# Gated-recurrence score products in blocks of 32 on quarters of TensorE's array, with the running samples' products moved behind them

## The chip, the cores and the metric

One core of a Trainium2 chip runs one program. The metric is the device time of one execution in microseconds (us); the number compared is the median of several runs. The engines are TensorE (PE, with its weight loads PEld), VectorE (DVE), ScalarE (ACT), GpSimd (POOL, all but unused here) and SyncE (SP), which issues the DMAs.

## The reference, cut to what matters

A two-layer trunk for 256 new tokens and 8 single-token running samples (264 columns in all), width 2048: layer 0 mixes with a Conformer convolution, layer 1 with an HGRN2 gated recurrence of 16 heads of 128 x 128; each layer ends in a convolutional FFN of width 5632. The change is in the recurrence:

```
G = jnp.cumsum(gc, axis=1)
decay = jnp.exp(G[:, :, None] - G[:, None, :])            # where s <= t
A = jnp.einsum('bthk,btshk,bshk->bths', qc, decay, kc)    # scores
o = jnp.einsum('bths,bshv->bthv', A, vc) + (qc * jnp.exp(G)) @ S
S_new = jnp.exp(G_last)[..., None] * S + (kc * jnp.exp(G_last - G)).T @ vc
```

For a running sample with one token it is S = f * S + k v and o = q S, followed by an RMS norm per head and a gate.

## The kernel before, in words

**Wide products.** Every weight matrix comes in tiles of 2048 x 128 (1 MB, one DMA each). ACT rounds a tile to `wh` (L137), DVE makes the rest `wl` (L149), and PE multiplies in three products per 128 rows: `wh` x high part (L179), `wh` x low part (L180), `wl` x high part (L181), each 128 x 128 by 264 columns. A call of `slot` is one such tile: 16 x 3 = 48 wide products into one PSUM bank. Four tiles (`NATIVE`) go in plain fp32 instead (L176).

**Order.** PE, ACT and DVE run exactly in the order in which the code is written. `slot` first writes its 48 products and then takes one turn of a list: functions registered with `later(n, ...)` run n turns later, first those marked `first`, then the splits of coming weights (`wh` before, `wl` after the plain functions), then those marked `last`. So what PE does in a turn stands behind that slot's wide products; what DVE and ACT do in it runs beside them.

**A head.** Heads go through three slots each: `hf` (forget gate), `hq` (query), `hi` (value); behind the heads in `GATE_AFTER` one gate slot `hg` is put in, and the seven remaining `hg` slots follow the last head. After a head's `hi` slot, `doubling` builds query/key pairs R[2], R[4], ... R[128] whose decays are taken to the middle of blocks of 2, 4, ... tokens. One turn later PE does `flip` (three transposes, L714 and L715) and `scores`: for seven levels (L750: the diagonal, then blocks of 1, 2, 4, 8, 16, 32 tokens) and four groups of 64 tokens a product of 64 keys by 64 queries, all levels side by side in `pl` (two PSUM banks); then the 128-token block (L753), two 64 x 64 products for the 64-token level (L756), and two transposes (L759), all into `pa`. A turn later `select` copies the parts of `pa` (ACT, L765 to L768), multiplies `pl` with a 0/1 mask and sums over levels (DVE, L769 and L772), and `place` copies the sums into the score matrix AT (ACT, L777). `outputs` (L800 to L804) follows a turn later.

**Samples.** `sample_state` (DVE, L792, eight instructions, interleaved with the head's norm) updates the head's states `sm` four turns behind the head's first turn, and `sample_outputs` (PE, L813, eight products of 32 columns of `alone` by 128) reads them a turn later, into one bank `pos` that all heads share. After the last head, `pos` is copied, transposed (L878), squared, summed over partitions (L886), and `sample_norm` (DVE, L891 to L894) scales it. Then `samples_gated` (L925) multiplies with the gates, and the first `ho` slot (plain fp32, L176) reads the result `o2`.

An fp32 product leaves two records in the trace, each with a weight load of its own; a transpose and a wide product leave one.

Of the kernel before, what the change touches and what calls it, by code (L numbers as in the profile page):

```python
# [8 lines left out]
F32 = mybir.dt.float32  # L9
# [3 lines left out]
ALU = mybir.AluOpType  # L13
# [4 lines left out]
P = 128  # L18
# [6 lines left out]
HEADS = 16  # L25
# [21 lines left out]
LOADS = 4  # L47
TE = 17

GATE_AFTER = (3, 4, 6, 7, 9, 10, 12, 13, 15)  # L50
# [10 lines left out]
def kernel(ctx: ExitStack, tc: tile.TileContext, a: dict):  # L61
# [6 lines left out]
    wp = ctx.enter_context(tc.tile_pool(name="wp", bufs=3))  # L68
    ps = ctx.enter_context(tc.tile_pool(name="ps", bufs=5, space=PSUM))

    def bank(name):
        return ps.tile([P, 512], F32, tag="pt", name=name)
# [86 lines left out]
    def later(slots, fn, last=False, first=False):  # L159

        todo[slots][0 if first else 2 if last else 1].append(fn)
# [452 lines left out]
    with ExitStack() as ph:  # L614
# [5 lines left out]

        mask = cst[:, P:].rearrange("p (o n) -> p o n", o=1).to_broadcast((P, 2, len(LV) * 64))
        AT = [h1.tile([P, 2, P], F32, tag=f"AT{i}", name=f"AT{i}") for i in range(2)]
        for t in AT:
            vec.memset(t[64:, :, :64], 0.0)
        gss = h1.tile([P, HEADS, NB], F32, tag="gss", name="gss")
# [115 lines left out]
        def scores(h):  # L741
            d = heads[h]
            R, qk, K = d["R"], d["qk"], d["K"]
            pl = d["pl"] = ps.tile([P, 2, 512], F32, tag="pl", name=f"pl{h}", bufs=1)
            for l, b in enumerate(LV):
                for hf in range(2):
                    for i in range(2):
                        s = (2 * hf + i) * 64
                        key, query = (qk[:, 2, :], qk[:, 0, :]) if b == 0 else (R[b][:, 1, :], R[b][:, 0, :])
                        pe.matmul(pl[i * 64 : i * 64 + 64, hf, l * 64 : (l + 1) * 64], key[:, s : s + 64], query[:, s : s + 64],  # L750
                                  start=True, stop=True)
            pa = d["pa"] = bank(f"pa{h}")
            pe.matmul(pa[:, :P], R[128][:, 1, :P], R[128][:, 0, P:SEQ], start=True, stop=True)  # L753
            for hf in range(2):
                s = hf * P
                pe.matmul(pa[:64, P + hf * 64 : P + (hf + 1) * 64], R[64][:, 1, s : s + 64], R[64][:, 0, s + 64 : s + P],  # L756
                          start=True, stop=True)
            for i, k in enumerate((K, R[128][:, 1, P:SEQ])):
                pe.transpose(pa[:, (2 + i) * P : (3 + i) * P], k, ident)  # L759

        def select(h):
            d = heads[h]
            pa, pl, W = d.pop("pa"), d.pop("pl"), AT[h % 2]
            Kt = d["Kt"] = hp.tile([P, 2, P], F32, tag="Kt", name=f"Kt{h}", bufs=1)
            act.copy(Kt, pa[:, 2 * P :].rearrange("p (i k) -> p i k", i=2))  # L765
            act.copy(W[:64, :, 64:], pa[:64, P : 2 * P].rearrange("p (o t) -> p o t", o=2))
            A1 = d["A1"] = hp.tile([P, P], F32, tag="A1", name=f"A1_{h}", bufs=1)
            act.copy(A1, pa[:, :P])  # L768
            vec.tensor_tensor(out=pl[:, :, : len(LV) * 64], in0=pl[:, :, : len(LV) * 64], in1=mask, op=ALU.mult)  # L769
            lm = pl[:, :, : len(LV) * 64].rearrange("p o (l t) -> p o t l", t=64)  # L770
            wd = heads[h]["wd"] = hp.tile([P, 2, 64], F32, tag="wd", name=f"wd{h}", bufs=1)
            vec.tensor_reduce(out=wd, in_=lm, axis=AX.X, op=ALU.add)  # L772

        def place(h):
            for i in range(2):
                r = slice(i * 64, i * 64 + 64)
                act.copy(AT[h % 2][r, :, r], heads[h]["wd"][r])  # L777

# [144 lines left out]
        def samples_gated(lo, hi):  # L923
            assert all(heads[h]["gated"] for h in range(lo, hi))
            vec.tensor_tensor(out=o2[:, lo:hi, SEQ:], in0=o2[:, lo:hi, SEQ:], in1=gss[:, lo:hi, :], op=ALU.mult)  # L925

        for name, h in HGRN:
# [9 lines left out]
            elif name == "hi":  # L937
# [10 lines left out]
                later(4, lambda h=h: sample_state_and_norm(h))  # L948
                later(5, lambda h=h: sample_outputs(h), last=True)
                later(5, lambda h=h: normed(h))  # L950
                later(6, lambda h=h: flop(h), last=True)
                later(7, lambda h=h: columns(h), first=True)
                if h == HEADS - 1:
                    later(6, sample_rows, first=True)
                    later(6, sample_columns, last=True)
                    later(7, sample_squares, first=True)
                    later(7, sample_sum, last=True)
                    later(8, sample_norm, first=True)
                    later(8, lambda: samples_gated(0, HEADS - 2), last=True)
                    later(8, lambda: samples_gated(HEADS - 2, HEADS), last=True)  # L960
# [18 lines left out]
    with ExitStack() as ph:  # L979
# [10 lines left out]

        pl = ps.tile([P, 2, 512], F32, tag="pl", name="p_y", bufs=1)
        pt = ps.tile([P, 512], F32, tag="st", name="p_ss", bufs=1)
# [9 lines left out]
        for i in range(2):  # L1002
            turn_back(i, 1, pl[:, i, :])
        steps, r = [], []
# [112 lines left out]
```

## Time and profile before

| | us |
|---|---|
| median of 3 runs | 2479.26 (2478.76 to 2480.55) |
| the profiled execution | 2478.74 |
| its span, first to last instruction | 2477.0 |
| PE busy | 2446.4 (99%) |
| DVE busy | 1759.9 (71%) |
| ACT busy | 1110.7 (45%) |
| mean granted TensorE clock | 0.996 of full |

Busy time is the union of an engine's instructions. A PE record is as long as the product's way through the array; successive products overlap, so the distance between starts, not the length, is what a product costs. The recurrence's slots run from about 1131 to 1594 us.

### The profile page before, as it was taken

Reading aid. Unit: us, or ns where it says so; the run is one execution under the profiler, and the core shown is the slowest. Engines: PE = TensorE matmul, PEld = TensorE weight load, DVE = VectorE, ACT = ScalarE, POOL = GpSimd, SP = SyncE. Lnnn points to the kernel's source line nnn. Section 1 sums busy time; section 2 is a strip of 40 time slices with the busy share of each in tenths; the row PEclk is TensorE's granted clock in tenths of the full one; section 3 lists DMA queues with packets and bytes.
Section 4 is the critical chain, followed back from the end, with each engine's and each line's share of the span. In section 5 each row is a group of like instructions: output and inputs, shape, how many; then the busy total and the mean of one; then the engine's idle time right before and its main releaser. Section 6 shows DMA issues by size and latency. Waiting matters only on the chain.

```text
span 2477.0 us, 46795 instructions
## 1 busy us (share of the span) xinstructions
PE 2446.4 (99%) x19878; PEld 2391.7 (97%) x19878; DVE 1759.9 (71%) x3087; ACT 1110.7 (45%) x1759; POOL 0.2 (0%) x4
## 2 busy tenths in 40 slices
PE   8999899999999999999999999899999999999998
PEld 7888899999999999999999999899999999999998
DVE  8999867766566567568887888657767657656655
ACT  1112645444344344345655665444444444435434
POOL 0000000000000000000000000000000000000000
PEclk9999999999999999999999999999999999999999
DMA  7444445554554554555655655455555455455453
GB/s 270 150 153 142 169 173 204 176 182 156 202 187 161 182 196 164 180 182 197 232 190 202 222 208 199 161 182 199 176 187 173 158 205 180 158 201 186 164 176 129
DMA packets 78129, 452.92 MB, mean 183 GB/s; under 512 B 8544, under 2 KB 13024, under 8 KB 39008
## 3 DMA queue, kind: packets, MB, share of 16 engines
q1 hardware_dynamic: 77920, 449.94, 51.6%
q8 instruction: 155, 2.54, 0.4%
q14 instruction: 54, 0.44, 0.0%
HBM read 436.31 MB, written 15.50 MB: 182 GB/s over the span
## 4 chain that ended last, share of the span: by engine, by line
PE 99%; DVE 1%; issue 0%; DMA 0%; ACT 0%; ACTq 0%; SPq 0%; DVEq 0%
PE p_up L181 14%; PE p_up L179 14%; PE p_up L180 14%; PE p_pw L176 10%; PE p_dn L181 7%; PE p_dn L180 7%; PE p_dn L179 7%; PE p_hi L179 1%; PE p_hg L179 1%; PE p_hf L179 1%; PE p_hq L179 1%; PE p_hf L181 1%; PE p_hg L181 1%; PE p_hq L181 1%; PE p_hi L181 1%; PE p_hi L180 1%
## 5 line engine op out<-in xcount | busy, mean ns | idle before, releaser
L179 PE MATMUL p_up<-h_ffn,wh_up 128*128 128x264 f32 x2816 | 801.1, 284 | 0.0
L181 PE MATMUL p_up<-h_ffn,wl_up 128*128 128x264 f32 x2816 | 800.7, 284 | 0.0
L180 PE MATMUL p_up<-l_ffn,wh_up 128*128 128x264 f32 x2816 | 797.5, 283 | 0.0
L149 DVE TENSOR_TENSOR wl_up<-w_up,wh_up 128x2048 fp32r<-128x2048 f32 x176 | 403.5, 2293 | 231.9 <-ACT wh_up L137 231.9
L137 ACT CAST wh_up<-w_up 128x2048 fp32r<-128x2048 f32 x176 | 335.9, 1909 | 505.9 <-PE p_up L180 446.8
L179 PEld LDWEIGHTS p_up<-h_ffn,wh_up 128*128 128x128 f32 x2816 | 530.1, 188 | 0.1
L181 PEld LDWEIGHTS p_up<-h_ffn,wl_up 128*128 128x128 f32 x2816 | 530.0, 188 | 0.0
L180 PEld LDWEIGHTS p_up<-l_ffn,wh_up 128*128 128x128 f32 x2816 | 529.6, 188 | 0.1
L181 PE MATMUL p_dn<-gh,wl_dn 128*128 128x264 f32 x1408 | 400.8, 285 | 0.0
L179 PE MATMUL p_dn<-gh,wh_dn 128*128 128x264 f32 x1408 | 400.3, 284 | 0.0
L180 PE MATMUL p_dn<-gl,wh_dn 128*128 128x264 f32 x1408 | 400.1, 284 | 0.0
L137 ACT CAST wh_dn<-w_dn 128x1408 fp32r<-128x1408 f32 x128 | 175.9, 1374 | 325.9 <-PE p_dn L180 243.8
L149 DVE TENSOR_TENSOR wl_dn<-w_dn,wh_dn 128x1408 fp32r<-128x1408 f32 x128 | 208.1, 1626 | 108.3 <-ACT wh_dn L137 108.3
L180 PEld LDWEIGHTS p_dn<-gl,wh_dn 128*128 128x128 f32 x1408 | 265.3, 188 | 0.0
L181 PEld LDWEIGHTS p_dn<-gh,wl_dn 128*128 128x128 f32 x1408 | 264.7, 188 | 0.0
L179 PEld LDWEIGHTS p_dn<-gh,wh_dn 128*128 128x128 f32 x1408 | 264.6, 188 | 0.0
L176 PE MATMUL p_pw<-xg,w_pw 128*128 128x264 f32 x960 | 213.9, 386 | 0.0
L176 PEld LDWEIGHTS p_pw<-xg,w_pw 128*128 128x128 f32 x960 | 182.4, 190 | 31.2
L567 DVE SCALAR_TENSOR_TENSOR C<-H,par,C 128x255 f32<-128x255 f32 x352 | 169.1, 480 | 6.3
L278 DVE TENSOR_TENSOR x<-x,p_dn 128x264 f32<-128x264 f32 x128 | 54.9, 429 | 111.9 <-PE p_dn L181 111.9
L561 DVE TENSOR_TENSOR H<-p_up,rstd_ffn 128x264 f32<-128x264 f32 x176 | 76.1, 432 | 78.3 <-PE p_up L181 78.3
L562 ACT ACTIVATE C<-H,par 128x264 f32<-128x264 f32 x176 | 105.5, 600 | 13.9 <-DVE H L561 13.9
(316 smaller groups left out, 4007.9 us busy)
## 6 DMA issues: line engine op xcount, KB each, us to landing
w_up<-in_up SPq DMA_DIRECT2D x176, 1024.0 KB
w_dn<-in_dn SPq DMA_DIRECT2D x128, 704.0 KB
w_pw<-in_pw SPq DMA_DIRECT2D x47, 1024.0 KB
w_hf<-in_hf SPq DMA_DIRECT2D x16, 1024.0 KB
w_hq<-in_hq SPq DMA_DIRECT2D x16, 1024.0 KB
w_hi<-in_hi SPq DMA_DIRECT2D x16, 1024.0 KB
w_hg<-in_hg SPq DMA_DIRECT2D x16, 1024.0 KB
w_ho<-in_ho SPq DMA_DIRECT2D x16, 1024.0 KB
```

The costliest lines, as they stand in the source:

```text
L137: act.copy(wh[:, :kk, :], raw[key][:, :kk, :])
L149: vec.tensor_tensor(out=wl[:, :kk, :], in0=raw.pop(key)[:, :kk, :], in1=wh.bitcast(F32)[:, :kk, :], op=ALU.subtract)
L176: pe.matmul(pt[:, :T], wh[:, k, :], full[k], start=(k == 0), stop=last)
L179: pe.matmul(pt[:, :T], wh[:, k, :], rh, start=(k == 0), stop=False)
L180: pe.matmul(pt[:, :T], wh[:, k, :], rl, start=False, stop=False)
L181: pe.matmul(pt[:, :T], wl[:, k, :], rh, start=False, stop=last)
L278: vec.tensor_tensor(out=x[n], in0=x[n], in1=pt[:, :T], op=ALU.add)
L561: vec.tensor_tensor(out=h, in0=pt[:, :T], in1=rstd, op=ALU.mult)
L562: act.activation(cc, h, AF.Identity, scale=wv[:, j, 2:3], bias=pcol("ffn_b", layer * 2 * FT + j))
L567: vec.scalar_tensor_tensor(out=cc[:, d:SEQ], in0=h[:, : SEQ - d], scalar=wv[:, j, 2 - d : 3 - d], in1=cc[:, d:SEQ], op0=ALU.mult, op1=ALU.add)
```

## The change

Scores of the diagonal and of the levels 1 to 16 are made in blocks of 32 keys by 32 queries: six levels, each eight blocks, of which four consecutive ones go to the four 32-column quarters of the array (output partitions 0, 32, 64, 96). `pl` shrinks to 384 columns in one PSUM bank, the free bank goes to the common pool (five banks to six), and mask and sum work on 384 instead of 896 columns. The 32-token level becomes four 32 x 32 products into free columns of `pa` (quarters 0 and 2), the 64-token level four products of 32 keys by 64 queries (one to a quarter). Behind them stand the samples' products of the head before (`sample_outputs(h - 1)`), then the 128-token product and the transposes. `select` and `place` have more, smaller copies. The last head's samples and the chain behind them move a turn forward.

```
-    ps = ctx.enter_context(tc.tile_pool(name="ps", bufs=5, space=PSUM))
+    ps = ctx.enter_context(tc.tile_pool(name="ps", bufs=6, space=PSUM))
...
+        by_level = cst[:, P:].rearrange("p (l t) -> p l t", t=64)
+        for r in (B, 3 * B):
+            act.copy(by_level[r : r + B, :NL, :B], by_level[r : r + B, :NL, B:])
+        mask = by_level[:, :NL, :B].unsqueeze(1).to_broadcast((P, 2, NL, B))
...
-            pl = d["pl"] = ps.tile([P, 2, 512], F32, tag="pl", name=f"pl{h}", bufs=1)
-            for l, b in enumerate(LV):
+            pl = d["pl"] = ps.tile([P, 2, NL, B], F32, tag="pl", name=f"pl{h}", bufs=1)
+            pa = d["pa"] = bank(f"pa{h}")
+            for l, b in enumerate(LV[:NL]):
+                key, query = (qk[:, 2, :], qk[:, 0, :]) if b == 0 else (R[b][:, 1, :], R[b][:, 0, :])
                 for hf in range(2):
-                    for i in range(2):
-                        s = (2 * hf + i) * 64
-                        key, query = (qk[:, 2, :], qk[:, 0, :]) if b == 0 else (R[b][:, 1, :], R[b][:, 0, :])
-                        pe.matmul(pl[i * 64 : i * 64 + 64, hf, l * 64 : (l + 1) * 64], key[:, s : s + 64], query[:, s : s + 64],
-                                  start=True, stop=True)
-            pa = d["pa"] = bank(f"pa{h}")
+                    for i in range(P // B):
+                        s = hf * P + i * B
+                        pe.matmul(pl[i * B : i * B + B, hf, l, :], key[:, s : s + B], query[:, s : s + B], start=True, stop=True)
+            for hf in range(2):
+                for r in range(0, P, 64):
+                    s = hf * P + r
+                    pe.matmul(pa[r : r + B, P + 64 + hf * B : P + 64 + hf * B + B], R[B][:, 1, s : s + B],
+                              R[B][:, 0, s + B : s + 64], start=True, stop=True)
+            for hf in range(2):
+                for i in range(2):
+                    r, s = 2 * hf + i, hf * P
+                    pe.matmul(pa[r * B : r * B + B, P : P + 64], R[64][:, 1, s + i * B : s + i * B + B],
+                              R[64][:, 0, s + 64 : s + P], start=True, stop=True)
+            if h > 0:
+                sample_outputs(h - 1)
             pe.matmul(pa[:, :P], R[128][:, 1, :P], R[128][:, 0, P:SEQ], start=True, stop=True)
-            for hf in range(2):
-                s = hf * P
-                pe.matmul(pa[:64, P + hf * 64 : P + (hf + 1) * 64], R[64][:, 1, s : s + 64], R[64][:, 0, s + 64 : s + P],
-                          start=True, stop=True)
...
-            act.copy(W[:64, :, 64:], pa[:64, P : 2 * P].rearrange("p (o t) -> p o t", o=2))
+            for hf in range(2):
+                act.copy(W[:64, hf, 64:], pa[hf * 64 : hf * 64 + 64, P : P + 64])
...
+            for r in range(0, P, 64):
+                act.copy(W[r : r + B, :, r + B : r + 64], pa[r : r + B, P + 64 : 2 * P].rearrange("p (o t) -> p o t", o=2))
+            vec.tensor_tensor(out=pl, in0=pl, in1=mask, op=ALU.mult)
...
-            for i in range(2):
-                r = slice(i * 64, i * 64 + 64)
-                act.copy(AT[h % 2][r, :, r], heads[h]["wd"][r])
+            for r in range(0, P, B):
+                act.copy(AT[h % 2][r : r + B, :, r : r + B], heads[h]["wd"][r : r + B])
...
-                later(5, lambda h=h: sample_outputs(h), last=True)
...
-                    later(6, sample_rows, first=True)
-                    later(6, sample_columns, last=True)
-                    later(7, sample_squares, first=True)
-                    later(7, sample_sum, last=True)
-                    later(8, sample_norm, first=True)
-                    later(8, lambda: samples_gated(0, HEADS - 2), last=True)
+                    later(4, lambda: sample_outputs(HEADS - 1), last=True)
+                    later(5, sample_rows, first=True)
+                    later(5, sample_columns, last=True)
+                    later(6, sample_squares, first=True)
+                    later(6, sample_sum, last=True)
+                    later(7, sample_norm)
+                    later(7, lambda: samples_gated(0, HEADS - 2), last=True)
```

Three places in the written order. First PE behind the `hq` slot of head 4, before: the samples' products of head 3 (`pos`), the transposes (`pv`), the levels (`pl`), and the rest (`pa`); each x4 or x8 is a run of products.

```order
L813 MATMUL pos<-sm_12255,alone_nv 32x128 x8
L714 MATMUL pv_13014<-cst,v_12895 128x128 x2
L715 MATMUL pv_13014<-cst,v_12895 8x128
L750 MATMUL pl_13018<-qk_12718 64x64 x8
L750 MATMUL pl_13018<-R_4_12831 64x64 x4
L750 MATMUL pl_13018<-R_4_12834 64x64 x4
L750 MATMUL pl_13018<-R_4_12923 64x64 x4
L750 MATMUL pl_13018<-R_4_12926 64x64 x4
L750 MATMUL pl_13018<-R_4_12929 64x64 x4
L753 MATMUL pa_13047<-R_4_12935 128x128
L756 MATMUL pa_13047<-R_4_12932 64x64 x2
L759 MATMUL pa_13047<-cst,K_12937 128x128
```

That is the form for the samples of 8 heads; for the other 8 heads they stand alone between the wide products of two slots, as here for head 0.

```order
L179 MATMUL p_hi_12006<-h_after_15_11264,wh_hi_11833 128x264
L180 MATMUL p_hi_12006<-l_after_15_11266,wh_hi_11833 128x264
L181 MATMUL p_hi_12006<-h_after_15_11264,wl_hi_11863 128x264
L813 MATMUL pos<-sm_11426,alone_acc 32x128 x8
L179 MATMUL p_hf_12102<-h_after_0_10582,wh_hf_11940 128x264
L180 MATMUL p_hf_12102<-l_after_0_10586,wh_hf_11940 128x264
```

After the change every head has one form. Here it is for head 1, with what each first instruction waits for (line numbers are those of the changed file: levels L757, 32-token level L761, 64-token level L766, samples L827, 128-token block L770, transposes L772).

```order
L757 MATMUL pl_12004<-R_1_11883 32x32 [waits DVE_49]
L757 MATMUL pl_12004<-R_1_11883 32x32 x7
L761 MATMUL pa_12005<-R_1_11886 32x32 [waits DVE_49,PE_49]
L761 MATMUL pa_12005<-R_1_11886 32x32 x3
L766 MATMUL pa_12005<-R_1_11889 32x64 [waits DVE_49]
L766 MATMUL pa_12005<-R_1_11889 32x64 x3
L827 MATMUL pos<-sm_11428,alone_acc 32x128 [waits DMAHW5_49,DVE_49]
L827 MATMUL pos<-sm_11428,alone_acc 32x128 [waits DVE_49] x7
L770 MATMUL pa_12005<-R_1_11892 128x128
L772 MATMUL pa_12005<-cst,K_11894 128x128
L772 MATMUL pa_12005<-cst,R_1_11892 128x128
```

The samples' products of head 0 have moved from their own place into head 1's block, which stands one slot earlier, and the change between 32-column quarters and the whole array now comes once in the block.

Second DVE at the end of the recurrence, before: the split of the second `ho` tile (`wl_ho`), the samples' norm (its first two and last two rows here), then the last gate.

```order
L149 TENSOR_TENSOR wl_ho_17530<-w_ho_17403,wh_ho_17525 128x2048
L891 TENSOR_SCALAR sample_two<-p_so 128x128
L211 TENSOR_SCALAR sample_two<-sample_two 128x128
L212 TENSOR_SCALAR sample_two<-sample_two 128x128
L214 TENSOR_TENSOR sample_sq<-sample_two 128x128
```

```order
L216 SCALAR_TENSOR_TENSOR sample_two<-sample_sq,sample_two 128x128
L894 TENSOR_TENSOR o_11284<-p_sc,sample_two 128x4x2x16
L654 TENSOR_TENSOR zg_17548<-p_hg_17467,rstd_after_2704 128x264
L866 SCALAR_TENSOR_TENSOR gsig_17550<-zg_17548,par,gsig_17550 128x264
L868 COPY gss<-gsig_17550 128x8
L869 TENSOR_TENSOR o_11284<-o_11284,gsig_17550 128x256
L925 TENSOR_TENSOR o_11284<-o_11284,gss 128x14x8
L925 TENSOR_TENSOR o_11284<-o_11284,gss 128x2x8
```

And after, from the end of the samples' norm on.

```order
L218 SCALAR_TENSOR_TENSOR sample_two<-sample_sq,sample_two 128x128
L908 TENSOR_TENSOR o_11286<-p_sc,sample_two 128x4x2x16
L880 SCALAR_TENSOR_TENSOR gsig_18023<-zg_18021,par,gsig_18023 128x264
L882 COPY gss<-gsig_18023 128x8
L883 TENSOR_TENSOR o_11286<-o_11286,gsig_18023 128x256
L151 TENSOR_TENSOR wl_ho_18044<-w_ho_17905,wh_ho_18025 128x2048
L939 TENSOR_TENSOR o_11286<-o_11286,gss 128x14x8
L660 TENSOR_TENSOR zg_18047<-p_hg_17969,rstd_after_2704 128x264
L880 SCALAR_TENSOR_TENSOR gsig_18049<-zg_18047,par,gsig_18049 128x264
L882 COPY gss<-gsig_18049 128x8
L883 TENSOR_TENSOR o_11286<-o_11286,gsig_18049 128x256
L939 TENSOR_TENSOR o_11286<-o_11286,gss 128x2x8
```

The norm has moved ahead of the split and of the last two gates, into the turn beside the last `hg` slot.

## Rows read from the trace of the kernel before

**Rows 1.** The page: part 1 (busy us, share of the span, instructions) and part 4 (the chain that ended last, shares by engine).
```profile
PE 2446.4 (99%) x19878; PEld 2391.7 (97%) x19878; DVE 1759.9 (71%) x3087; ACT 1110.7 (45%) x1759; POOL 0.2 (0%) x4
PE 99%; DVE 1%; issue 0%; DMA 0%; ACT 0%; ACTq 0%; SPq 0%; DVEq 0%
```

**Rows 2.** The waits of PE: which line waited for whom, us in total, times, longest.
```profile
PE p_ho L176 <- issue: 6.3, 1, 6.3
...
PE p_sc L878 <- ACT sample_rows L874: 0.4, 1, 0.4
```

**Rows 3.** A window over the recurrence: length, then busy us of PE, PEld, DVE, ACT and POOL (x instructions), granted PE clock, DMA share, GB/s.
```profile
1150.00:1564.00 414.00, 414.00 (x4210) 401.23 (x4209) 336.82 (x734) 247.91 (x587) 0.00 (x0) 1.00 0.57 206
```

**Rows 4.** PE in order of time around head 0's scores: start us, length us, line, tile, shape, records.
```profile
1156.07 0.29 PE L181 MATMUL p_hq<-h_after,wl_hq 128*128 128x264 f32 x1
...
1156.42 0.27 PE L715 MATMUL pv<-cst,v 128*8 128x128 f32 x1
1156.62 0.69 PE L750 MATMUL pl<-qk 128*64 128x64 f32 x16
1157.13 1.34 PE L750 MATMUL pl<-R 128*64 128x64 f32 x40
1158.40 0.49 PE L753 MATMUL pa<-R 128*128 128x128 f32 x2
1158.82 0.45 PE L756 MATMUL pa<-R 128*64 128x64 f32 x4
...
1159.36 0.27 PE L759 MATMUL pa<-cst,R 128*128 128x128 f32 x1
...
1159.59 0.28 PE L180 MATMUL p_hi<-l_after,wh_hi 128*128 128x264 f32 x1
```

**Rows 5.** The same around the samples' products of head 0, which stand alone.
```profile
1187.12 0.28 PE L181 MATMUL p_hi<-h_after,wl_hi 128*128 128x264 f32 x1
1187.33 0.65 PE L813 MATMUL pos<-sm,alone_acc 128*32 128x128 f32 x16
1187.91 0.39 PE L179 MATMUL p_hf<-h_after,wh_hf 128*128 128x264 f32 x1
1188.13 0.28 PE L180 MATMUL p_hf<-l_after,wh_hf 128*128 128x264 f32 x1
```

**Rows 6.** The same where head 3's samples' products stand directly ahead of head 4's transposes and scores.
```profile
1252.61 0.28 PE L181 MATMUL p_hf<-h_after,wl_hf 128*128 128x264 f32 x1
1252.82 0.64 PE L813 MATMUL pos<-sm,alone_nv 128*32 128x128 f32 x16
...
1256.85 0.28 PE L180 MATMUL p_hq<-l_after,wh_hq 128*128 128x264 f32 x1
```

**Rows 7.** Short windows over the samples' products of Rows 5: length, then busy us of PE, PEld and ACT for the tile `pos`, in brackets the records in flight in the window, clock, DMA share, GB/s.
```profile
1187.46:1187.49 0.03, 0.03 (x8) 0.03 (x8) 0.00 (x0) 1.00 0.00 0
1187.49:1187.57 0.08, 0.08 (x8) 0.08 (x4) 0.00 (x0) 1.00 0.87 358
1187.57:1187.60 0.03, 0.03 (x12) 0.03 (x8) 0.00 (x0) 1.00 0.33 137
```

**Rows 8.** The semaphore instructions of PE's sequencer in head 0's scores, for lines L750 and L753: shortest, median, longest in ns, first and last start in us.
```profile
L750 PEldq EVENT_SEMAPHORE  x2: 51/51/51, 1156.6 to 1156.8; - x2
...
L753 PEldq EVENT_SEMAPHORE  x1: 51/51/51, 1157.7 to 1157.7; - x1
```

**Rows 9.** DVE in order of time: the last of the eight state updates of head 0 and of head 5.
```profile
1178.27 0.34 DVE L792 SCALAR_TENSOR_TENSOR sm<-vb,ks,sm 128x128 f32<-128x128 f32 x1
...
1303.27 0.34 DVE L792 SCALAR_TENSOR_TENSOR sm<-vb,ks,sm 128x128 f32<-128x128 f32 x1
```

**Rows 10.** PE in order of time: the last transpose ahead of head 1's and of head 6's scores.
```profile
1178.34 0.27 PE L715 MATMUL pv<-cst,v 128*8 128x128 f32 x1
...
1304.49 0.27 PE L715 MATMUL pv<-cst,v 128*8 128x128 f32 x1
```

**Rows 11.** Groups of instructions by line: busy us in total, mean ns of one, idle time before them and its releaser.
```profile
L769 DVE TENSOR_TENSOR pl<-pl,cst 128x896 f32<-128x896 f32 x16 | 17.4, 1089 | 0.9 <-PE pl L750 0.9
...
L777 ACT COPY AT<-wd 64x128 f32<-64x128 f32 x32 | 9.7, 302 | 0.2
...
L766 ACT COPY AT<-pa 64x128 f32<-64x128 f32 x16 | 4.2, 261 | 0.0
```

**Rows 12.** All engines in order of time at the end of the recurrence.
```profile
1585.29 2.29 DVE L149 TENSOR_TENSOR wl_ho<-w_ho,wh_ho 128x2048 fp32r<-128x2048 f32 x1 [0.78 <-ACT wh_ho L137]
...
1587.21 0.29 PE L181 MATMUL p_hg<-h_after,wl_hg 128*128 128x264 f32 x1
...
1587.76 0.29 DVE L891 TENSOR_SCALAR sample_two<-p_so 128x128 f32<-128x128 f32 x1 [0.18 <-PE p_so L886]
...
1591.77 0.42 DVE L654 TENSOR_TENSOR zg<-p_hg,rstd_after 128x264 f32<-128x264 f32 x1
...
1592.67 0.49 DVE L866 SCALAR_TENSOR_TENSOR gsig<-zg,par,gsig 128x264 f32<-128x264 f32 x1 [0.49 <-ACT gsig L861]
...
1593.62 0.35 DVE L925 TENSOR_TENSOR o<-o,gss 128x112 f32<-128x112 f32 x2
1593.99 7.20 PE L176 MATMUL p_ho<-o,w_ho 128*128 128x264 f32 x22 [6.27 <-issue]
```

**Rows 13.** A window over the start of the first `ho` slot, columns as in Rows 3.
```profile
1594.00:1598.00 4.00, 4.00 (x9) 3.15 (x10) 3.23 (x10) 4.00 (x13) 0.00 (x0) 0.50 0.00 0
```

More of the change, by code (lines that the diff above doesn't have):

```diff
@@ L48 @@
 TE = 17
+B = 32
+NL = len(LV) - 1
 GATE_AFTER = (3, 4, 6, 7, 9, 10, 12, 13, 15)
@@ L619 @@
         later(0, st.finish, last=True)
-        mask = cst[:, P:].rearrange("p (o n) -> p o n", o=1).to_broadcast((P, 2, len(LV) * 64))
+        by_level = cst[:, P:].rearrange("p (l t) -> p l t", t=64)
+        for r in (B, 3 * B):
+            act.copy(by_level[r : r + B, :NL, :B], by_level[r : r + B, :NL, B:])
+        mask = by_level[:, :NL, :B].unsqueeze(1).to_broadcast((P, 2, NL, B))
         AT = [h1.tile([P, 2, P], F32, tag=f"AT{i}", name=f"AT{i}") for i in range(2)]
         for t in AT:
-            vec.memset(t[64:, :, :64], 0.0)
+            vec.memset(t, 0.0)
         gss = h1.tile([P, HEADS, NB], F32, tag="gss", name="gss")
@@ L765, in select @@
             act.copy(Kt, pa[:, 2 * P :].rearrange("p (i k) -> p i k", i=2))
-            act.copy(W[:64, :, 64:], pa[:64, P : 2 * P].rearrange("p (o t) -> p o t", o=2))
+            for hf in range(2):
+                act.copy(W[:64, hf, 64:], pa[hf * 64 : hf * 64 + 64, P : P + 64])
             A1 = d["A1"] = hp.tile([P, P], F32, tag="A1", name=f"A1_{h}", bufs=1)
             act.copy(A1, pa[:, :P])
[L769 to L772, printed above, removed]
+            for r in range(0, P, 64):
+                act.copy(W[r : r + B, :, r + B : r + 64], pa[r : r + B, P + 64 : 2 * P].rearrange("p (o t) -> p o t", o=2))
+            vec.tensor_tensor(out=pl, in0=pl, in1=mask, op=ALU.mult)
+            wd = heads[h]["wd"] = hp.tile([P, 2, B], F32, tag="wd", name=f"wd{h}", bufs=1)
+            vec.tensor_reduce(out=wd, in_=pl.rearrange("p o l t -> p o t l"), axis=AX.X, op=ALU.add)
         def place(h):
-            for i in range(2):
-                r = slice(i * 64, i * 64 + 64)
-                act.copy(AT[h % 2][r, :, r], heads[h]["wd"][r])
+            for r in range(0, P, B):
+                act.copy(AT[h % 2][r : r + B, :, r : r + B], heads[h]["wd"][r : r + B])
         def decay(h):
@@ L989, in turn_back @@
                 pe.transpose(pt[:, j * P : (j + 1) * P], x[4 * c + j][:, i * P : (i + 1) * P], ident)
-        pl = ps.tile([P, 2, 512], F32, tag="pl", name="p_y", bufs=1)
+        pl = ps.tile([P, 512], F32, tag="pl", name="p_y", bufs=1)
         pt = ps.tile([P, 512], F32, tag="st", name="p_ss", bufs=1)
@@ L1002 @@
         for i in range(2):
-            turn_back(i, 1, pl[:, i, :])
+            turn_back(i, 1, bank(f"p_y{i}_1") if i else pl)
         steps, r = [], []
```

## The prediction

> **What bounds the kernel now.** I read the page first: PE is busy for 99% of the span, and the chain that ended last is 99% PE [rows 1]. Then the waits: the only ones of PE inside the part that changes are one of 6.3 us ahead of the first `ho` slot and one of 0.4 us for the samples' transpose [rows 2]. In the window over the recurrence PE is busy in all of 414 us while DVE has 337 (81%) and ACT 248 (60%) [rows 3]. So whatever shortens PE's own sequence there shortens the run, as long as no other engine begins to hold PE up. Then I read PE's sequence in order of time, for what a block between two slots costs.
>
> **What a block costs now.** A wide product costs 0.12 us, start to start. Head 0's block reaches from 1156.07 + 0.12 to 1159.59 - 0.12: 3.28 us [rows 4]. Its parts:
> - Transposes: 0.34 (the last starts at 1156.42 and takes 0.11).
> - Into 64-column halves of the array: 0.14, up to the first product at 1156.67 (its record starts at 1156.62 but is 0.05 longer than those behind it).
> - Levels: 28 products are 56 records, in pairs on the two halves. The 40 of R start between 1157.13 and 1158.25 (0.22 before the group's end): 19 steps of 0.0587, so 28 x 0.0587 = 1.64.
> - The rest, 1.16: whole array for the 128-token block, halves for the 64-token level, whole array for the transposes. Each change costs 0.14 to 0.21 in which nothing streams; the four records of L756 go one after the other on one half at 0.0587 each, 0.23; a record of 128 columns on the whole array costs 0.11.
>
> The samples' products alone cost 1188.13 - 1187.12 - 0.24 = 0.77 [rows 5]: 0.12 into quarters, four rounds of 0.11, 0.21 back. In the short windows four records are in flight, eight between 1187.46 and 1187.49, no new one in the next 0.08, four more in the 0.03 after that [rows 7]: the quarters work at the same time, and four products start within 0.03 us. Where both stand together the block has 1256.85 - 1252.61 - 0.24 = 4.00 [rows 6].
>
> **The change on PE.** A round of four records of 32 columns is not in the trace. A round costs 0.0587 at 64 columns and 0.11 at 128, so 0.0008 per column; at 32 that gives 0.033. Bounds: 0.026 (the streaming of 32 columns alone, by that slope) and 0.0587 (no shorter than at 64 columns, which would cost 24 x 0.026 = 0.6 a head, 9.9 in all); what issue can add is a rival below. I take 0.033, on the line through the two rows that are there. New block: transposes 0.34, into quarters 0.12, 96 records in 24 rounds 0.79, 32-token level in four rounds on two quarters 0.13, 64-token level 2 x 0.0587 = 0.12, samples 0.44, back 0.21, 128-token block 0.22, transposes 0.22: 2.59 us. Of six changes of the array's form two are left.
> - Seven heads whose predecessor's samples stood alone: 3.28 + 0.77 - 2.59 = 1.46 each, 10.2.
> - Eight where they stood together: 4.00 - 2.59 = 1.41 each, 11.3.
> - Head 0, with no samples behind it: 3.28 - 2.15 = 1.13. The last head's samples stay alone: nothing.
>
> Together **-22.6**.
>
> Against that, PE's sequencer gets an extra semaphore instruction where a product waits for two things: about 17 in all (L761 in nine heads, the samples in eight). Two such instructions stand at most 0.2 us apart in head 0 [rows 8] and cost nothing there, the queue ahead being full. In the new block a round is half as long. Bounds 0 and 17 x 0.2 = 3.4; I take 0.05 each, nearer to the row that shows no cost: **+0.9**.
>
> **DVE, ACT, banks.** Mask and sum shrink from 896 to 384 columns; the mask's 1.09 [rows 11] should halve, and so the sum: DVE loses about 1.1 us a head and stays near 81% of a shorter stretch. ACT's copies grow: AT from 0.26 to four of some 0.2, `place` from two of 0.30 to four of 0.25 or so; by these rows about +1 us a head, 265 of 391 us. That hides beside the next slot's 48 products (5.8 us), since `outputs` reads AT only a slot later; without that cover it would be up to 16 us. Two mask copies and larger memsets come once. The sixth common bank can only let PE start earlier; no PE wait for a bank is there to win. The sample-state DMAs are released earlier and move no step of PE.
>
> **The new wait.** In seven heads the samples' products come a slot earlier, in the same turn as the state they read. Their LDWEIGHTS stands ahead of the 128-token block and the next slot's wide products, so a late state holds all of PE. Head 5's last update ends at 1303.61 and the last transpose ahead of head 6's scores starts at 1304.49; head 0's ends at 1178.61 against 1178.34 [rows 9, 10]. The products come 0.11 + 0.12 + 0.79 + 0.13 + 0.12 = 1.27 later, so 2.1 and 1.0 us are left. PE reaches head 1's block 1.1 earlier than now (head 0's gain), so that slack is near nothing once; I book 0, at most 0.2.
>
> **The end.** Now the samples' norm starts when PE's last `hg` slot is over (1587.76) and holds DVE until 1591.77; then come the last gate and 2.22 us later the first `ho` product, 6.66 us behind the last wide product's end at 1587.33 [rows 12]. After the change p_so stands ahead of the last slot: PE needs 0.44 for it and the last head's transposes, then 5.8 for the slot, ending 6.2 behind the start. DVE in that time: p_so at about 0.65, norm 4.0, gate 0.95 (1592.67 to 1593.62), split 2.29, samples 0.2: 8.1. Then last gate and path to `ho`, 2.1: 10.2. So 4.0 us of idleness remain; the stall goes from the norm to DVE being a split late. Gain 6.66 - 0.22 (p_so moves into PE's busy time) - 4.0 = 2.4, and the 0.4 wait of [rows 2] goes, since the transpose no longer waits for the last head's: **-2.8**.
>
> The granted clock is 0.50 over the first 4 us of `ho` [rows 13]: half speed (1.2 of 2.4 GHz) behind the idle 6.27 us. Those 4.2 us cost about 2.1. Behind 4.0 us of idleness it may stay at full (-2.1) or fall later and cost as much again inside the `ho` slot (+2.1); the idleness being shorter, I take a little off: **-0.4**.
>
> **Sum.** -22.6 + 0.9 - 2.8 - 0.4 = -24.9. The profiled execution took 2478.74, span 2477.0; the median is 2479.26, within 0.02% of it. 2479.26 - 24.9 = 2454.4, rounded to 2455 since the unbooked costs are all above.
>
> **A rule that speaks against it.** The windows show four starts in 0.03 us, but only in bursts of four with 0.08 between [rows 7]. The Trainium skill (TensorE: Matmul & The Clock Gate, "Wait — 56ns, not 53.3ns?") says that start-to-start never drops below about 25 ns however small a product is. By that rule, taken over all quarters, the 128 records of the quarter part would need 3.2 us in place of 1.48 and the run would come out near 2482; the starts of [rows 7] disagree unless it holds within a quarter only. Which it is at 0.033 a round no row here shows.
>
> **The rivals.**
> - *Issue sets the pace.* Head 0's 40 records of R were issued between the second semaphore instruction (1156.8) and the one ahead of L753 (1157.7): at most 0.022 each [rows 8]. The queue ran 0.7 us ahead then, some 18 to 20 records. If 0.022 is the true price, 78 of the 96 level records take 1.72 in place of 0.79 and the two levels behind 0.1 more: 16 x 1.03 = 16.5 lost, 2471. Same place, other cause: only two quarters at once, 24 x 0.033 more a head, 12.7, 2467. For it: no row shows so many records in sequence; against it: [rows 7].
> - *No gain.* The samples' records at 0.11 / 4 = 0.027 each [rows 7], taken as a fixed price of a record, with the queue's lead of 18: 110 x 0.027 - 1.48 = 1.5 a head, 24 us, 2479. The near figure of the levels (1.64 / 56 = 0.029) speaks for it, the 0.022 of [rows 8] against. The floor that the Trainium skill states would end in this case.
> - *Slower.* The levels' 0.029 [rows 4] as a fixed price, and no lead of the queue: 128 x 0.029 - 1.48 = 2.2 a head, 36 us, 2490. Without the lead it decides from 0.024 on, where the gain is gone. For and against it stands the same as for the last one; besides, the lead is seen in [rows 8].
> - *PE not the bound.* DVE at 81% comes too late for the states or for `wl` in the shorter turns: 1 us in each of seven heads, 2462. For it: the 0.27 of head 0; against it: DVE loses 1.1 a head.
>
> **How the numbers follow.** Forecast with its own range 2446 to 2462: 0.70 (lower end: rounds at 0.026 -2.7, full clock -1.7, no semaphore cost -0.9, the 32-token level beside its neighbours -2; upper end: the late DVE or semaphores at 0.2). Issue or two quarters, 2462 to 2474: 0.15. No gain, 2474 to 2484: 0.07. Slower: 0.05. Below 2446: 0.03. The range 2446 to 2468 takes half of the second case in and leaves about 2 in 10 out. Within 0.2% (5 us, about what a measurement tells from no change): 0.07, faster 0.88, slower 0.05.
>
> **What would show it.** Level records (L757) in fours, 0.033 a round, 0.8 us a head; a block of 2.6; no L813-like gap between two slots; PE idle ahead of `ho` near 4.0; busy PE over the recurrence still 100%. Wrong would be: more than 0.015 us per level record, a wait of L827 for DVE, or idle PE within the slots.

## The result, and the profile after

The changed kernel takes 2461.53 us (median, 2461.28 to 2461.79), the kernel before 2479.53 beside it: a ratio of 0.9927, 95% interval 0.9910 to 0.9944. That is 18.0 us less. The forecast was 2455 in a range of 2446 to 2468: the sign and the range hold, but the time is 6.5 us above the forecast, and the terms inside the sum are further off than that: two errors of opposite sign partly cancel.

The profiled execution took 2461.53, its span is 2459.8 (2477.0 before, so 17.2 to be explained). First the page of after: busy times and the chain that ended last, as in [rows 1].

```profile
PE 2432.9 (99%) x20710; PEld 2378.5 (97%) x20710; DVE 1742.7 (71%) x3087; ACT 1125.7 (46%) x1841; POOL 0.2 (0%) x4
PE 82%; DVE 11%; ACT 5%; issue 2%; DMA 0%; DVEq 0%; SPq 0%; ACTq 0%
```

Part 1 reads as before. The second line does not: the chain was PE for 99% and is now PE for 82%, with 16% on DVE and ACT. Something other than PE sets the pace in part of the run.

PE in order of time around head 3's block, an undisturbed one (compare [rows 4, 6]).

```profile
1220.49 0.29 PE L183 MATMUL p_hf<-h_after,wl_hf 128*128 128x264 f32 x1
...
1220.83 0.27 PE L721 MATMUL pv<-cst,v 128*8 128x128 f32 x1
1221.03 0.46 PE L757 MATMUL pl<-qk 128*32 128x32 f32 x32
1221.31 0.72 PE L757 MATMUL pl<-R 128*32 128x32 f32 x62
...
1222.09 0.64 PE L827 MATMUL pos<-sm,alone_acc 128*32 128x128 f32 x15
...
1223.32 0.28 PE L182 MATMUL p_hq<-l_after,wh_hq 128*128 128x264 f32 x1
```

By the prediction's way of reading, the block takes 1223.32 - 1220.49 - 0.24 = 2.59 us, the very figure of the forecast. The 96 level records run from 1221.03 to about 1221.86: 0.0087 each, four to a round of 0.035.

Now head 6's block, in all engines' order of time, with the first and last of head 5's eight state updates (L806) on DVE, and the same samples' products in head 9's block.

```profile
1296.71 0.29 PE L183 MATMUL p_hf<-h_after,wl_hf 128*128 128x264 f32 x1
1296.81 0.34 DVE L806 SCALAR_TENSOR_TENSOR sm<-vb,ks,sm 128x128 f32<-128x128 f32 x1
...
1297.05 0.27 PE L721 MATMUL pv<-cst,v 128*8 128x128 f32 x1
...
1298.37 1.78 PE L827 MATMUL pos<-sm,alone_nv 128*32 128x128 f32 x15
...
1299.34 0.35 DVE L806 SCALAR_TENSOR_TENSOR sm<-vb,ks,sm 128x128 f32<-128x128 f32 x1
...
1300.75 0.28 PE L182 MATMUL p_hq<-l_after,wh_hq 128*128 128x264 f32 x1
...
1377.30 2.41 PE L827 MATMUL pos<-sm,alone_acc 128*32 128x128 f32 x14
```

The products that take 0.64 in head 3 take 1.78 here and 2.41 in head 9: they go out two by two behind the updates, which come 0.33 apart. Before, head 5's last update ended 0.9 ahead of head 6's last transpose [rows 9, 10]; now it ends 2.6 behind it. The block takes 1300.75 - 1296.71 - 0.24 = 3.80. Heads 9, 12 and 15 read in the same way give 5.10, 5.05 and 5.08, head 1 2.91, all others 2.59 to 2.74. Over 2.59 that is 9.4 us in all.

A part of the loss stands inside slots: six slots, whose `wl` products wait, are 0.3 to 0.6 us longer than the others, 2.8 us in all by the starts of their products. PE's waits show the three `hg` slots among them.

```profile
PE p_hg L183 <- DVE wl_hg L151: 1.0, 3, 0.4
```

What DVE waits for over the recurrence: before (two lines, 1150 to 1564), then after (1150 to 1555).

```profile
DVE wl_hg L149 <- ACT wh_hg L137: 24.8, 11, 4.0
DVE wl_hf L149 <- ACT wh_hf L137: 21.9, 13, 4.0
```

```profile
DVE wl_hg L151 <- ACT wh_hg L139: 31.0, 12, 4.0
DVE wl_hf L151 <- ACT wh_hf L139: 30.7, 14, 4.0
```

DVE's idle time is not free time. After the change 76.4 of its 84 us stand ahead of its rest `wl`, waiting for ACT's cast (59.3 of 77 before), although DVE is busy for less. And before, DVE still waited for PE, 4.6 us in all; after, no wait of DVE for PE is left: here PE no longer sets DVE's pace. The place is this, in the turn of head 4's `hf` slot (ACT and DVE in order of time):

```profile
1276.06 0.43 DVE L660 TENSOR_TENSOR zf<-p_hf,rstd_after 128x264 f32<-128x264 f32 x1
1276.52 0.42 ACT L671 ACTIVATE qk<-zf 128x264 f32<-128x264 f32 x1 [9.30 <-DVE zf L660]
...
1277.71 0.85 ACT L674 ACTIVATE G<-zf,lb,lbc 128x256 f32<-128x256 f32 x1
1278.35 0.35 ACT L676 ACTIVATE fs<-zf,lb,lbc 128x8 f32<-128x8 f32 x1
1278.60 1.90 ACT L139 CAST wh_hg<-w_hg 128x2048 fp32r<-128x2048 f32 x1
1280.53 2.29 DVE L151 TENSOR_TENSOR wl_hg<-w_hg,wh_hg 128x2048 fp32r<-128x2048 f32 x1 [4.04 <-ACT wh_hg L139]
```

DVE makes `zf`, ACT's five forget operations need it (2.1 us), the cast of the next tile is written behind them (1.9), and DVE's rest needs the cast. DVE goes in written order, so it stands still for 4.04 us while everything behind it, the state updates among them, moves back. ACT had before that waited 9.30 us for `zf`, with nothing to do.

How much room that chain had is seen in the time of three heads, from the last transpose of head 9 to that of head 12. PE in order of time, before (L715) and after (L721):

```profile
1384.78 0.27 PE L715 MATMUL pv<-cst,v 128*8 128x128 f32 x1
...
1465.12 0.27 PE L715 MATMUL pv<-cst,v 128*8 128x128 f32 x1
```

```profile
1375.30 0.27 PE L721 MATMUL pv<-cst,v 128*8 128x128 f32 x1
...
1454.88 0.27 PE L721 MATMUL pv<-cst,v 128*8 128x128 f32 x1
```

80.34 became 79.58. PE's own work in it shrank by 1.46 + 2 x 1.41 = 4.3; only 0.8 came through.

Last the end (all engines in order of time; a window over the first `ho` slot with columns as in [rows 13]).

```profile
1576.31 2.28 DVE L151 TENSOR_TENSOR wl_ho<-w_ho,wh_ho 128x2048 fp32r<-128x2048 f32 x1
1576.90 0.28 PE L183 MATMUL p_hg<-h_after,wl_hg 128*128 128x264 f32 x1
1578.51 0.27 DVE L939 TENSOR_TENSOR o<-o,gss 128x112 f32<-128x112 f32 x1
1578.84 7.39 PE L178 MATMUL p_ho<-o,w_ho 128*128 128x264 f32 x32 [1.65 <-DVE o L939]
1580.14 0.17 DVE L882 COPY gss<-gsig 128x8 f32<-128x8 f32 x1
```

```profile
1580.00:1584.00 4.00, 4.00 (x19) 3.42 (x19) 2.97 (x11) 4.00 (x10) 0.00 (x0) 1.00 0.56 229
```

The first `ho` product starts 1578.84 - 1576.90 = 1.94 behind the start of the last wide product, where it was 1593.99 - 1587.21 = 6.78 [rows 12]: 4.8 us. It does not wait for the last gate at all, which ends after it has started. Behind this idle time of 1.65 the granted clock stays at 1.00 (it was 0.50 behind 6.27 us [rows 13]), which is worth half of 4 us, 2.0: the slot's native products take 7.3 us now and took 9.4.

The span's account: blocks -22.5 (head 0 at 2.20, heads 1 to 15 at 2.59) and -0.3 in small blocks of the tail, +9.4 waits for states, +2.8 waits for `wl`, +0.3 before the recurrence, end -4.8, clock -2.0: -17.1 of the 17.2 seen.

### The profile page after: what moved, and what is told of

The parts are those of the page before. It is cut to its first block, busy times and chain, and to the rows that moved or that the text cites. A ratio compares the mean times of both kernels' runs of the same rounds, so it can differ in the third digit from the quotient of the medians.

```text
span 2459.8 us, 48528 instructions
## 1 busy us (share of the span) xinstructions
PE 2432.9 (99%) x20710; PEld 2378.5 (97%) x20710; DVE 1742.7 (71%) x3087; ACT 1125.7 (46%) x1841; POOL 0.2 (0%) x4
## 3 DMA queue, kind: packets, MB, share of 16 engines
q8 instruction: 162, 2.65, 0.4%
## 4 chain that ended last, share of the span: by engine, by line
PE 82%; DVE 11%; ACT 5%; issue 2%; DMA 0%; DVEq 0%; SPq 0%; ACTq 0%
PE p_up L183 14%; PE p_up L181 14%; PE p_up L182 14%; PE p_pw L178 10%; PE p_dn L183 7%; PE p_dn L182 7%; PE p_dn L181 7%; DVE R L703 3%; DVE wl_hi L151 1%; PE p_ho L181 1%; PE p_ho L182 1%; PE p_ho L183 1%; PE p_pw L182 1%; PE p_pw L181 1%; PE p_pw L183 1%
```

## The experiments

Theory A: a serial chain sets the pace, wherever the samples' products stand: DVE makes `zf` (the expectations call this "normal"), ACT runs its forget operations and then its cast, DVE makes the rest `wl`. Theory B: DVE has slack (71% busy), and only the new place of the products is at fault.

**The two parts apart.** The end alone is the kernel before with the tail of the diff; the scores alone is the changed kernel with

```
-                    later(4, lambda: sample_outputs(HEADS - 1), last=True)
+                    later(5, lambda: sample_outputs(HEADS - 1), last=True)
...
-                    later(7, sample_norm)
+                    later(8, sample_norm, first=True)
```

> The kernel before with one part of the change: the last head's samples' products and the chain behind them a turn earlier, scores and all other samples as before. If the end's gain is independent of the rest, PE's idleness ahead of `ho` falls from 6.3 to about 1.7 us and the clock stays at full over the `ho` slot: 2479.5 - 4.8 - 2.0 = 2472.7. The prediction's own figure for this part was -3.2: 2476.3, with 4 us of idleness.

> The changed kernel with the last head's samples and the chain behind them where they stood before; the blocks of 32 and the samples' products of the other heads as changed. If the two parts of the change add up, this is slower than the changed kernel by what the end alone gave: 7.6 us by the run with the end alone, 6.9 by the traces (idle time 4.8, clock 2.0), so 2468 to 2469.5. If the end is worth only what the prediction booked (3.2), 2464.7. If the late states also reach the end, so that the parts do not add up, outside 2467 to 2470.5.

Measured: 2471.55 for the end (0.9969, 0.9958 to 0.9981; 7.6 us) and 2468.99 for the scores (0.9959, 0.9945 to 0.9973; 10.4 us). They add up to the 18.0 of both, so the end was booked at less than half of its worth (2.8 + 0.4), and it has nothing to do with the late states. PE's wait ahead of `ho`, end alone and then scores alone:

```profile
PE p_ho L176 <- DVE o L925: 1.6, 1, 1.6
```

```profile
PE p_ho L178 <- DVE o L939: 6.2, 1, 6.2
```

**The samples' products back at their own place** (all heads but the last).

```
-            if h > 0:
-                sample_outputs(h - 1)
...
+                if h < HEADS - 1:
+                    later(5, lambda h=h: sample_outputs(h), last=True)
```

> The changed kernel, but the samples' products stand in their old place, a turn behind the state they read. On PE that costs 0.77 - 0.44 = 0.33 us a head, 5.0 us for 15 heads. Theory A (the round trip DVE - ACT - DVE paces the recurrence; the late states are only where it shows): PE's waits of 9.4 us behind L827 come back as waits for `wl` or for R, and the time stays at 2460 to 2463. Theory B (DVE has slack; only the place of the products is wrong): the 9.4 us go, nothing takes their place, and the time falls by 4.4 to 2457.

Measured 2459.75 (0.9920, 0.9905 to 0.9935), just outside A's interval and 2.8 above B's 2457. The blocks no longer wait for states, but PE's waits inside the slots are other and longer ones:

```profile
PE p_hi L183 <- DVE wl_hi L151: 1.4, 2, 0.7
...
PE p_hq L183 <- DVE wl_hq L151: 1.0, 2, 0.6
...
PE p_hg L183 <- DVE wl_hg L151: 0.7, 2, 0.3
```

Of the 9.4 us only a little came back as waits: six slots are now 4.6 us longer in all, against 2.8. By the total alone neither theory holds. The pace says more. PE in order of time, head 9's and head 12's last transpose:

```profile
1376.10 0.27 PE L721 MATMUL pv<-cst,v 128*8 128x128 f32 x1
...
1455.40 0.27 PE L721 MATMUL pv<-cst,v 128*8 128x128 f32 x1
```

These three heads take 79.30 us, nearly the 79.58 of the changed kernel, though PE alone would do them in 77.1, as it does heads 3 to 6 in this run. So late in the recurrence the pace is the same wherever the products stand, as A has it; in the old place PE only runs longer before the waits begin.

**The cast first**, in the changed kernel and in the kernel before:

```
-                later(0, lambda h=h, pt=pt: forget(h, pt), first=h > 0)
+                later(0, lambda h=h, pt=pt: forget(h, pt))
```

> The changed kernel, but in the turns of the `hf` slots ACT rounds the coming weight tile before the five forget-gate instructions instead of behind them. It changes nothing on PE. Theory A: DVE's waits ahead of wl_hf (30.7 us for 14 of them, all for ACT's cast) shrink below 10 us, DVE runs ahead, and PE's waits for the states and for `wl` (together 11.5 us) nearly go: 2449 to 2453. Theory B: the samples' products still stand behind states of the same turn, and the time stays within 2 us of 2461.5.

> The kernel before, with ACT's five forget operations behind its cast of the coming tile instead of ahead of it. Theory A (the serial chain DVE normal, ACT forget, ACT cast, DVE rest holds PE up only in the changed kernel, because PE is faster there): PE is busy without a gap in the kernel before, so nothing is to be won, 2478.5 to 2479.7. Rival (the cast's place is a gain by itself, with or without the change): about 10 us less, 2469.

Measured: 2451.43 (0.9888, 0.9874 to 0.9903) and 2479.35 (1.0000, 0.9991 to 1.0010). Ten us from one word that changes ACT's order and no work, and nothing from the same word in the kernel before. B falls. What DVE waits for with the cast first, 1150 to 1547:

```profile
DVE zq L660 <- PE p_hq L183: 18.7, 8, 3.3
DVE wl_hf L151 <- ACT wh_hf L139: 14.9, 8, 2.3
...
DVE wl_hg L151 <- ACT wh_hg L139: 3.5, 7, 1.5
```

The wait for `wh_hg` falls from 31.0 to 3.5, that for `wh_hf` only to 14.9 (A had it below 10), and DVE waits for PE again, 18.7 us ahead of `zq`: PE is the bound once more. Head 9's last transpose starts at 1375.34, head 12's at 1451.55; three heads take 76.21, against 80.34 - 4.3 = 76.0 by PE's work.

**More work for DVE**: the mask product three times instead of once, 1.12 us a head.

```
-            vec.tensor_tensor(out=pl, in0=pl, in1=mask, op=ALU.mult)
+            for _ in range(3):
+                vec.tensor_tensor(out=pl, in0=pl, in1=mask, op=ALU.mult)
```

> The changed kernel with the mask multiplied in three times instead of once (the result is the same, since the mask is 0 or 1): two more DVE instructions of 0.56 us a head, about what the change took off DVE. Theory A: all of it lands in the time, 16 x 1.1 = 18 us, 2476 to 2480. Theory B: it counts only in the four heads that wait for a late state, 4 x 1.1 = 4.5 us, 2466.

Measured 2461.43 (0.9927, 0.9907 to 0.9947): no change, and both theories missed. The waits of DVE tell why:

```profile
DVE wl_hg L151 <- ACT wh_hg L139: 24.6, 10, 4.0
DVE wl_hf L151 <- ACT wh_hf L139: 21.0, 10, 4.0
```

32 x 0.57 = 18 us were added, and the waits for the casts shrank by about as much: 6.4 and 9.7 in these lines, and 2.5 ahead of `wl_hq`. The mask stands ahead of such a wait, so more of it fills the wait and less of it lengthens the wait. So A holds for the chain, not for DVE's sum of work, and in the changed kernel the halved mask bought nothing.

**The chain longer**: one of the five forget operations done twice (booked at 0.64 us), in the changed kernel and in the one with the cast first.

```
-            act.activation(gated_by(1), z[:, :SEQ].rearrange("p (n s) -> p n s", s=2), AF.Identity,
+            for _ in range(2):
+                act.activation(gated_by(1), z[:, :SEQ].rearrange("p (n s) -> p n s", s=2), AF.Identity,
```

> The changed kernel with one of ACT's five forget operations (the 128 x 256 one, 0.64 us from start to start) done twice in every head, so that the chain from DVE's normal to ACT's cast to DVE's rest is 0.64 us longer; the result is the same. Theory A (this chain sets the pace): the extra time comes back in the run, in full 16 x 0.62 = 9.9 (2471), or only in the two of three heads ahead of a late state, 6.5 (2468): 2466 to 2471. Theory B (ACT at 46% and DVE at 71% have slack, only the samples' products stand too early): 2461.5 to 2462.5.

> The kernel with the cast first, and with ACT's 128 x 256 forget operation done twice in every head (0.64 us), as in the run with the long chain; the result is the same. Theory A (the chain DVE normal, ACT forget, ACT cast, DVE rest set the pace; with the cast first the forget operations are no longer in it): the extra work hides, 2451.4 to 2453. Rival (any 0.64 us of ACT in a turn comes back, wherever it stands): 2461 to 2465, as the same addition cost the changed kernel 13.5.

Measured: 2474.99 (0.9983, 0.9974 to 0.9993), 13.5 us more than the changed kernel, and 2451.04 (0.9889, 0.9874 to 0.9904), nothing more than the cast first alone. The same work on the same engine costs 13.5 us in the chain and nothing beside it. It is more than A's 6.5 to 9.9, since the added operation costs more than 0.64. ACT and DVE in order of time in the longer chain, at the place that is shown above for the changed kernel:

```profile
1283.66 1.75 ACT L675 ACTIVATE G<-zf,lb,lbc 128x256 f32<-128x256 f32 x2
...
1287.37 2.29 DVE L151 TENSOR_TENSOR wl_hg<-w_hg,wh_hg 128x2048 fp32r<-128x2048 f32 x1 [4.94 <-ACT wh_hg L139]
```

The two take 1.75 where one took 0.85, and DVE waits 4.94 instead of 4.04: 0.90 more. In the 15 heads where the cast stands behind them that makes 13.5. Nor is it the clock, though it did fall. One wait of PE in order of time, and the window behind it:

```profile
1364.32 0.39 PE L183 MATMUL p_hi<-h_after,wl_hi 128*128 128x264 f32 x1 [1.52 <-DVE wl_hi L151]
```

```profile
1364.30:1368.00 3.70, 3.68 (x18) 3.68 (x19) 0.31 (x1) 3.29 (x7) 0.00 (x0) 0.57 0.73 232
```

Behind that wait the granted clock is 0.57 over 3.7 us, and the wide products come every 0.22 us instead of 0.12. The same happened at 1446.5 (0.53 over 3.5 us). The last transposes of heads 9, 12 and 15, and by the same reading head 6's at 1302.62, tell what it cost:

```profile
1384.78 0.27 PE L722 MATMUL pv<-cst,v 128*8 128x128 f32 x1
...
1466.99 0.27 PE L722 MATMUL pv<-cst,v 128*8 128x128 f32 x1
...
1549.16 0.27 PE L722 MATMUL pv<-cst,v 128*8 128x128 f32 x1
```

Three heads take 82.16, 82.21 and 82.17; the first two stretches hold one fall of the clock each, the third none (1.00 throughout). So the slower products only filled time that PE would else have waited for the chain. Against the changed kernel's 79.58 that is 2.6 us, three times nearly 0.9.

**Both: the cast first, and the products back at their own place.**

> The changed kernel with the cast first and with the samples' products of all but the last head back at their own place a slot later. Theory A (the place of the products is right, the chain was too long): with the short chain nothing waits, and PE pays for the products' own changes of the array's form, 15 x 0.33 = 5 us more than cast first alone, less head 1's wait of 1.3: 2455 to 2456.5. Theory B (the place is what costs, whatever the chain): not slower than cast first alone, 2451.5 or less.

Measured 2456.33 (0.9909, 0.9894 to 0.9924): 4.9 more than the cast first alone, as A had it. With the short chain the new place of the products is worth the 0.33 us a head that PE saves there. With the long chain it costs 1.8 (2461.53 against 2459.75), because the lateness holds PE up earlier there. The chain itself costs 10.1 with the products in the new place and 3.4 in the old one.

**Quarter by quarter**: the cast first, with the 48 products of 32 x 32 ordered so that one quarter gets its twelve before the next begins.

```
-            for l, b in enumerate(LV[:NL]):
-                for hf in range(2):
-                    for i in range(P // B):
+            for i in range(P // B):
+                for l, b in enumerate(LV[:NL]):
+                    for hf in range(2):
```

> The kernel with the cast first, and with the 48 products of 32 x 32 of a head written quarter by quarter (12 products, 24 records, on one quarter before the next) and not going round the four quarters. If four quarters at once is what makes a record cost 0.008 us, one quarter alone takes 0.033 for each: 96 x (0.033 - 0.008) = 2.4 us a head, 16 heads 38 us, less some 1.3 of head 1's wait: 2488. At 0.025 a record on one quarter: 96 x 0.017 = 1.6 a head, 2476. If the rate of issue alone sets it and the order of the quarters does not matter: 2451.4.

Measured 2478.34 (0.9998, 0.9988 to 1.0007): 26.9 more, all of the change's gain gone with the same products in another order. PE in order of time in one block:

```profile
1225.50 0.44 PE L757 MATMUL pl<-qk 128*32 128x32 f32 x8
1225.77 0.58 PE L757 MATMUL pl<-R 128*32 128x32 f32 x13
1226.16 0.22 PE L757 MATMUL pl<-qk 128*32 128x32 f32 x1
...
1226.25 0.20 PE L757 MATMUL pl<-R 128*32 128x32 f32 x1
```

21 records in 0.66 us, 0.031 each on one quarter. That is near the 0.033 of my first case. I had it at 2488 mainly because I let no quarter start before the one ahead had ended. But the next quarter's first record (`qk`, 1226.16) starts ahead of the last three of this one (`R`, the last at 1226.25). That the time lies near the 2476 of the 0.025 case is luck.

**Head 0's samples alone again**, with the cast first.

```
-            if h > 0:
+            if h > 1:
                 sample_outputs(h - 1)
...
+                if h == 0:
+                    later(5, lambda h=h: sample_outputs(h), last=True)
```

> The kernel with the cast first, but head 0's samples' products (and only those) stand alone a slot later, as before the change. In the kernel with the cast first head 1's block takes 3.94 us where the others take 2.65, since head 0's states come 1.3 us late. If that wait goes and only the products' own changes of the array's form come back (0.33): 1.0 less, 2450.4. If the wait comes back elsewhere in head 1: 2451.4 to 2452.

Measured 2451.57 (0.9889, 0.9875 to 0.9904): nothing won, and the expectation's cause was wrong. I had taken the long block of head 1 from the profile of the cast first:

```profile
1180.98 0.64 PE L827 MATMUL pos<-sm,alone_acc 128*32 128x128 f32 x13 [0.89 <-issue]
```

It waits for "issue", not for DVE; head 0's states were done at 1175.9. That profiled execution took 2453.48, 2.0 more than its kernel's median: this block is 1.3 longer than the others, and a gap inside a later slot takes 0.7. In the run with the cast first and the longer chain the block takes 2.65, while a gap of 0.9 stands in the same later slot. What stopped the issue in head 1 that once, no run here shows.

## Why the prediction was right or wrong, point by point

- **Blocks, -22.6: right**, -22.5 by the trace. The round of four at 0.033 lay on the line through the 64 and 128 column rows; over all 96 records it is 0.035. The rivals that made issue the pace are refuted, and so is the rule that speaks against it, if taken over all quarters. The quarter-by-quarter run shows why the rate holds: four quarters work at once.
- **Semaphores, +0.9**: the 17 instructions are there (nine for L761, eight for L827), but their cost is not to be seen; the block with them takes the 2.59 of the sum without them. The bound at nothing was the right one.
- **"The new wait", booked at 0: this step failed**, by 9.4 us, and by 2.8 more inside the slots. I measured the slack of head 5's states against PE as it ran before (2.1 us), and took off PE's gain only once, for head 1. But PE gains 1.4 us in every head, and the states gain with it only if the chain that makes them has room. It had 0.8 us in three heads.
- **"DVE and ACT stay hidden", and the 81%**: the error under the one above. Of the 77 us in which DVE stood idle [rows 3], 46.7 were the two lines of waits for ACT shown above. A rival named this, "PE not the bound", at 1 us in each of seven heads; it was against it that DVE loses 1.1 us a head. The run with the thrice-made mask shows that this work was no part of what sets the pace, and the waits that did come cost 12.2 us, not 7.
- **ACT's copies, nothing**: ACT is busy for 15.0 us more, as booked (1 us a head). Their cost was not tried alone, but with the cast first the copies are all there, and PE's waits name DVE nowhere in the recurrence.
- **The end, -2.8, and the clock, -0.4: right in sign, undersized**; -4.8 and -2.0 by the trace, -7.6 by the medians of the run with the end alone (7.1 by the spans of the two traces, of which -0.3 stands in the small blocks). That the stall becomes DVE's late split was right; the step that failed is that I let `ho` wait for the last gate. Its first 14 products read only the 14 heads that are finished a gate earlier, and DVE reaches those right behind the split. So the idle time is 1.65 and not 4.0, and behind it the clock does not fall.
- **What would show it wrong** did: L827 waits for DVE, and wide products wait for `wl`. The time came out near the 2462 of the rival *PE not the bound* because a better end (3.6 us more) paid for part of a larger loss; that nearness, and with it the 6.5 us of distance to the forecast, is luck.

The version that beats both kernels is the change with the cast first, at 2451.4: below the forecast, since hardly any of the blocks' gain is waited away and the end gives more than was booked.

## What to carry to other kernels

Before an engine that is busy for 99% is made faster, ask of the others not how busy they are but what their idle time waits for. Idle time that waits for a neighbour, which itself waits for this engine, is part of a loop with a time of its own; compare that loop's time per period with the new period, and look for work in it that could stand elsewhere in the written order. And price a wait by when it ends for the first reader, not by the last gate in the list.

## What the runs showed of the hardware that was not expected

Small products overlap across column quarters only when those written near each other go to different quarters. Going round the four, a record of 32 columns starts every 0.0087 us over 96 in a row; on one quarter every 0.031. Written quarter by quarter, the next quarter starts only some three records early. So PE's records do not start strictly in the written order where quarters differ. The Trainium skill (TensorE: Matmul & The Clock Gate, "Wait — 56ns, not 53.3ns?") has about 25 ns as the least from start to start: the runs here agree with it within a quarter, where nothing was faster, and are at a third of it across four.

The clock can fall inside a slot. In the run with the longer chain two waits for `wl` of 1.52 us of idle time, which end at 1364.32 and 1446.52, were followed by 3.7 us at 0.57 and 3.5 us at 0.53 of full speed, near the lower of the two levels (1.2 of 2.4 GHz). A third wait of 1.52 us in the same run, which ends at 1528.69, was not, nor were two of about 1.2 us at 1282.15 and 1289.72. What tells them apart no run here settles. Neither fall made the run longer, since PE was waiting for another engine's chain there.
